# Four edits to the linear-attention stage of a hybrid decoder layer: the second pair's gate, the sum of x's two parts, the key transposes and the rule that hands out filler matmuls

## The chip, the cores and the metric

The kernel runs on one core of a Trainium2 chip. The metric is the device time of one execution in microseconds. Five engines work side by side, each in its own written order: TensorE (PE in the profile, with its weight loads as PEld), VectorE (DVE), ScalarE (ACT), GpSimd (POOL) and SyncE (SP), which issues nearly all DMAs.

## The reference

One decoder layer for 1024 prompt tokens and 64 sample tokens (8 sequences of 8), 1088 in all, in float32. Cut to what matters:

```python
xn   = rmsnorm(x, g_mix)
proj = xn @ w_in                      # qg kg vg r lr | qs ks vs
log_a = log_sigmoid(lr @ w_gup + b_g) / 16.0          # forget gate, 4 heads x 64 keys
S, o_g = gla_chunked(qg, kg, vg, log_a, s0, chunk)    # linear attention: S' = exp(b) S + k^T v
o_s  = dilated softmax attention of 8 heads (windows 128, 512, 2048)
o_g  = rmsnorm(o_g, g_gla) * silu(r)
h    = x + concat(o_g, o_s) @ w_out
y    = h + (silu(hn @ w_fg) * (hn @ w_fu)) @ w_fd      # hn = rmsnorm(h, g_ffn), width 2816
return rmsnorm(y, g_final), states, keys and values to keep
```

The gate's running sum `b = cumsum(log_a)` enters every product of queries and keys inside a chunk as `exp(b_t - b_s)`; the kernel cuts these products into levels, so that no exponent becomes large.

## The kernel before, in words

All products of float32 matrices are made of three matmuls on parts: a matrix is split into a high part `hi` (rounded by a copy) and a low part `lo` (the rest), and `mm3` (L201 to L203) adds hi·hi, hi·lo and lo·hi. `xhi` and `xlo` hold the transposed x in this way, 128 partitions by 8 blocks by 1088 tokens.

The program has these stages, with their times in the profiled execution: up to 60 us x is loaded, transposed and multiplied with the first two blocks of weights (queries and keys of the first pair of linear-attention heads); from 60 to about 310 us linear attention runs over two pairs of heads (`gla_heads`, g = 0 and 1); from about 310 to 675 us the softmax attention runs over four pairs (`attn_pair`, each about 88 us); then the output projection's second half and the norm, to about 780 us; then the feed-forward part to the end.

`gla_heads` walks three parts of the tokens: parts 0 and 1 are 512 prompt tokens each, part 2 the 64 sample tokens. In each part the levels h = 64, 32, 16, 8, 4, 2, 1 are gone through. A level takes two differences of `bT` on POOL (L618, L619), an exponent on ACT (L620), two products on DVE (tiles `Z`, L621, L622), and small matmuls on PE (L630 for the levels 64 and 32, L604 for the narrow ones, called bands). Then the state is brought forward: `kd` (POOL L647, ACT L649, DVE L650) is transposed on PE (L654), copied by ACT to `ktok` (L655), and multiplied with the values (L678). At the end of part 1 the outputs are scaled on DVE (L557) and transposed back (L692); part 2 has products of its own (L711, L713).

The gate (L366 to L381) is computed for both pairs ahead of `gla_heads(0)`: a matmul of `lrT` with `wg` (L371), then on DVE, ACT and again DVE to a scan (L380). Its tiles `z` and `mn` share two buffers (tag `qk`) with the queries and keys of the second pair, which a filler job writes later (L238).

Between these small matmuls PE is fed from a generator, `stream()`: 22 projection jobs of 12 steps of 6 matmuls each, then 32 steps of the output projection's first half. One step is called a yield here, and its matmuls filler. `tick` is called behind each level's, band's, state's and output's matmuls; it adds a weight from `GLA_W` and lets the generator run to a yield between `GLA_FROM[g]` and `GLA_TO[g]`, in proportion to the weights so far. Each of these pieces of filler may be issued only after the matmul it was called from (`issue_after`). Within these rules a scheduler that keeps a time line of its own sets the order of every engine's instructions.

x's parts are added again on POOL (L388) and written to `x_dram` by SP (L389), in pieces of 512, 512 and 64 tokens for each of 8 blocks, with two buffers, ahead of linear attention in the program and at low priority. The output projection reads `x_dram` much later (`xa`, from about 560 us on).

In the softmax attention SP's queue holds, for each pair, loads of a cache of keys (`in_cache_swa_k`), of values (`in_cache_swa_v`, in four tiles t = 0 to 3 with a small one per sequence), biases, and weights (`wraw`, L179) for the filler.

Of the kernel before, what the change touches and what calls it, by code (L numbers as in the profile page):

```python
# [2 lines left out]

# [1 line left out]

# [6 lines left out]
F32 = mybir.dt.float32  # L12
# [4 lines left out]
ALU = mybir.AluOpType  # L17
PSUM = bass.MemoryType.PSUM

P = 128  # L20
D = 1024
KT = D // P
# [3 lines left out]
TS = NB * NQ  # L26
TT = T + TS
# [10 lines left out]
NH = TT // 4  # L38
# [4 lines left out]
GLA_W = (1.0, 1.75, 0.75, 1.0)  # L43
# [60 lines left out]
def hymba_layer(  # L104
# [7 lines left out]
    nc = tc.nc  # L112
# [3 lines left out]
    pool = nc.gpsimd  # L116
    dma = nc.sync.dma_start
# [12 lines left out]
    x_dram = dram.tile([P, KT, TT], F32, name="x_dram")  # L130
# [9 lines left out]
    ident = const.tile([P, P], F32, name="ident")  # L140
# [65 lines left out]
    xhi = xpool.tile([P, KT, TT], F32R, name="xhi")  # L206
    xlo = xpool.tile([P, KT, TT], F32R, name="xlo")
# [142 lines left out]
    gla = open_pool("gla", side="left")  # L350
# [13 lines left out]
    pool.memset(reset[:, :T].rearrange("p (c t) -> p c t", t=P)[:, :, 0:1], 0.0)  # L364
    pool.memset(reset[:, T:].rearrange("p (c t) -> p c t", t=NQ)[:, :, 0:1], 0.0)
    bT = []  # L366
    for g in range(2):
        z = gla.tile([P, TT], F32, tag="qk", name="z", bufs=2)
        for c0, n in CHUNKS:
            ps = bank("S")  # L370
            mm(out=ps[:, :n], lhsT=wg[:, g * P : g * P + P], rhs=lrT[0:32, c0 : c0 + n], start=True, stop=True)  # L371
            vec.tensor_scalar(out=z[:, c0 : c0 + n], in0=ps[:, :n], scalar1=bg[:, g : g + 1], scalar2=None, op0=ALU.add)
        mn = gla.tile([P, TT], F32, tag="qk", name="mn", bufs=2)
        vec.tensor_scalar(out=mn, in0=z, scalar1=0.0, scalar2=None, op0=ALU.min)
        vec.scalar_tensor_tensor(out=z, in0=mn, scalar=2.0, in1=z, op0=ALU.mult, op1=ALU.subtract)
        act(out=z, in_=z, func=AF.Exp)
        act(out=z, in_=z, func=AF.Ln, bias=1.0)
        vec.tensor_tensor(out=mn, in0=mn, in1=z, op=ALU.subtract)
        b = gla.tile([P, TT], F32, tag="bT", name="bT", bufs=2)
        vec.tensor_tensor_scan(out=b, data0=reset, data1=mn, initial=0.0, op0=ALU.mult, op1=ALU.add)  # L380
        bT.append(b)  # L381


    with tc.high_priority(offset=-LOW):
        for k in range(KT):
            for lo, n in ((0, 512), (512, 512), (1024, TS)):
                xt = gla.tile([P, 512], F32, tag="xt", name="xt", bufs=2)[:, :n]
                pool.tensor_tensor(out=xt, in0=xhi[:, k, lo : lo + n].bitcast(F32), in1=xlo[:, k, lo : lo + n].bitcast(F32), op=ALU.add)  # L388
                dma(out=x_dram[:, k, lo : lo + n], in_=xt)  # L389

    ggh = gla.tile([P, 4], F32, name="ggh")
    vec.tensor_scalar(out=ggh, in0=gg, scalar1=0.5, scalar2=None, op0=ALU.mult)
# [144 lines left out]
    def gla_heads(g, q, k, V, Vs):  # L537
        ticks = [0]

        def tick(ins, kind):  # L540
            ticks[0] += GLA_W[kind]
            all_ = 20 * GLA_W[0] + 8 * GLA_W[1] + 2 * GLA_W[2] + 2 * GLA_W[3]
            fill_behind(ins, GLA_FROM[g] + (GLA_TO[g] - GLA_FROM[g]) * min(1, ticks[0] / all_))

        b = bT[g]
# [25 lines left out]
        for part in range(3):  # L571
            lo = part * W
            n = W if part < 2 else TS
            step = P if part < 2 else NQ
            ncmb = 4 if part < 2 else 1
            qp, kp, bp = q[:, lo : lo + n], k[:, lo : lo + n], b[:, lo : lo + n]
            levels = ((64, 32) if part < 2 else ()) + (LEVELS if part < 2 else LEVELS[2:])
            npart = P if part < 2 else TS
# [19 lines left out]
            def banded(ZL, ZR, mi):  # L598
                for i in range(2):
                    ps = columns(i, ncmb * 32)  # L600
                    for c in range(ncmb):
                        for j in range(nj):
                            sl = slice(c * P + 32 * j, c * P + 32 * j + 32)
                            ins = mm(out=ps[32 * j : 32 * j + 32, c * 32 : c * 32 + 32],  # L604
                               lhsT=ZL[64 * i : 64 * i + 64, sl], rhs=ZR[64 * i : 64 * i + 64, sl],
                               start=True, stop=True)
                    m = masks[:npart, mi, :].unsqueeze(1).broadcast_to([npart, ncmb, 32])
                    vec.copy_predicated(
                        out=comp[:, i * ncmb : (i + 1) * ncmb, :], mask=m.bitcast(U32),
                        data=ps[:npart].rearrange("p (x t) -> p x t", t=32),  # L610
                    )
                tick(ins, 0)

            for h in levels:
                Z = tmp("Z", 3)[:, :n]
                bv, zv = view(bp, h), view(Z, h)
                ref = bv[:, :, 0, h - 1 : h].broadcast_to([P, n // (2 * h), h])
                pool.tensor_tensor(out=zv[:, :, 0, :], in0=ref, in1=bv[:, :, 0, :], op=ALU.subtract)  # L618
                pool.tensor_tensor(out=zv[:, :, 1, :], in0=bv[:, :, 1, :], in1=ref, op=ALU.subtract)  # L619
                act(out=Z, in_=Z, func=AF.Exp, scale=1.0 / 16.0)  # L620
                vec.tensor_tensor(out=zv[:, :, 0, :], in0=view(kp, h)[:, :, 0, :], in1=zv[:, :, 0, :], op=ALU.mult)  # L621
                vec.tensor_tensor(out=zv[:, :, 1, :], in0=view(qp, h)[:, :, 1, :], in1=zv[:, :, 1, :], op=ALU.mult)  # L622
                if h <= 16:
                    banded(Z, Z, LEVELS.index(h))
                else:
                    for i in range(2):
                        pv = columns(i, ncmb * h).rearrange("p (x t) -> p x t", t=h)
                        for c in range(ncmb):
                            for a in range(0, P, 2 * h):
                                ins = mm(out=pv[a : a + h, c, :],  # L630
                                   lhsT=Z[64 * i : 64 * i + 64, c * P + a : c * P + a + h],
                                   rhs=Z[64 * i : 64 * i + 64, c * P + a + h : c * P + a + 2 * h],
                                   start=True, stop=True)
                        for a in range(0, P, 2 * h):
                            vec.tensor_copy(out=AT[a : a + h, i * ncmb : (i + 1) * ncmb, a + h : a + 2 * h], in_=pv[a : a + h])
                    tick(ins, 0)
            banded(kp, qp, len(LEVELS))
            for j in range(nj):
                act(out=AT[32 * j : 32 * j + 32, :, 32 * j : 32 * j + 32], in_=comp[32 * j : 32 * j + 32], func=AF.Copy)
# [5 lines left out]
            kd = tmp("kd")[:, :n]  # L645
            last = bp.rearrange("p (c t) -> p c t", t=step)[:, :, step - 1 : step].broadcast_to([P, n // step, step])
            pool.tensor_tensor(out=kd.rearrange("p (c t) -> p c t", t=step), in0=last,  # L647
                               in1=bp.rearrange("p (c t) -> p c t", t=step), op=ALU.subtract)
            act(out=kd, in_=kd, func=AF.Exp, scale=1.0 / 16.0)  # L649
            vec.tensor_tensor(out=kd, in0=kp, in1=kd, op=ALU.mult)  # L650
            kps = bank("T")
            ktok = tmp("ktok")
            for c in range(ncmb):
                nc.tensor.transpose(out=kps[:npart, c * P : c * P + P], in_=kd[:, c * P : c * P + npart], identity=ident)  # L654
            act(out=ktok[:npart, : ncmb * P], in_=kps[:npart, : ncmb * P], func=AF.Copy)  # L655

            ssg = gla.tile([P, 8], F32, tag="ssg", name="ssg", bufs=2)
# [106 lines left out]
    PF = {m: [att.tile([P, 2, P], F32, name=f"PF{i}{m}") for i in range(2)] for m in (P, 64)}  # L764
    for a in (Vf[0][64:, 1], Vf[1][64:, 1], PF[64][0][64:], PF[64][1][64:]):
        pool.memset(a, 0.0)

    def attn_pair(p):
        fs = slice(p * P, (p + 1) * P)
# [49 lines left out]
        ticks = [0]  # L819
# [85 lines left out]
        for gq in range(NTT // 2):  # L905
            Ps = [scores(2 * gq), scores(2 * gq + 1)]
            outputs(gq, Ps)
            for _ in range(4):
                next(sample, None)
        for _ in sample:  # L910
# [545 lines left out]
```

## Time and profile before

| what | value |
|---|---|
| three runs | 1564.93, 1574.18, 1579.67 us (median 1574.18) |
| the profiled execution | 1570.21 us |
| its span, and TensorE's mean granted clock | 1568.4 us, 0.973 |
| PE busy | 1476.7 us (94%), 13459 matmuls |
| DVE busy | 989.7 us (63%) |
| ACT busy | 593.1 us (38%) |
| POOL busy | 587.3 us (37%) |

The profiled execution lies 1.8 us above its span and 4 us below the median of the three runs. Busy shares are means over stages that differ: PE is close to full in the feed-forward part and has most of its gaps in linear attention, between 90 and 125 us and around 145 and 246 us, and near 680 us. The granted clock stands in the profile's window view as a share of 2.4 GHz; 0.50 is 1.2 GHz.

### The profile page before, as it was taken

The page shows a single profiled execution, that of the slowest core. Times are in us where ns is not written, and L with a number is a line of the kernel's source. Part 1 is how long each engine was busy: PE and PEld are TensorE (multiplying, and loading weights), DVE is VectorE, ACT ScalarE, POOL GpSimd, SP SyncE. Part 2 cuts the span into 40 slices and gives each one's busy share as a digit, 9 for nine tenths or more (in the row PEclk, how much of TensorE's full clock was granted, in tenths as well). Part 3 has the DMA queues.
Part 4 walks back from the last instruction along what each step waited for, and adds up shares of the span by engine and source line. Part 5 has one row for each costly group of instructions (what it writes and reads, how often), then busy time and mean ns, then how long its engine had stood idle before and what let it go on. Part 6 is the DMA issues. An engine that isn't in the chain of part 4 may idle for free. (4 is left out here: it accounts for less than half of the span.)

```text
span 1568.4 us, 32306 instructions
## 1 busy us (share of the span) xinstructions
PE 1476.7 (94%) x13459; PEld 1328.9 (85%) x13459; DVE 989.7 (63%) x1669; ACT 593.1 (38%) x1006; POOL 587.3 (37%) x413
## 2 busy tenths in 40 slices
PE   6979999999999999969889999999988999999996
PEld 6867877886777766569889999999988999999996
DVE  5486586543233324246577777777788887767766
ACT  4143233245242526323443333333335433333432
POOL 1494342041212010024475543345543455444521
PEclk9988999999999999989999999999999999999998
DMA  5321121164443527575543332232332633323211
GB/s 156 90 81 31 30 70 43 43 189 117 125 116 110 156 89 228 151 230 165 174 132 95 108 94 81 82 108 83 108 110 91 185 95 108 94 81 100 90 41 58
DMA packets 242211, 170.23 MB, mean 109 GB/s; under 512 B 17648, under 2 KB 228496, under 8 KB 242064
## 3 DMA queue, kind: packets, MB, share of 16 engines
q1 hardware_dynamic: 237856, 167.95, 36.0%
q8 instruction: 106, 1.74, 0.5%
q10 hardware_dynamic: 4208, 0.21, 0.2%
q14 instruction: 41, 0.34, 0.1%
HBM read 144.66 MB, written 23.46 MB: 107 GB/s over the span
## 5 line engine op out<-in xcount | busy, mean ns | idle before, releaser
L1113 POOL TENSOR_TENSOR raw<-raw 128x1024 f32<-128x1024 f32 x88 | 260.6, 2969 | 366.2 <-DVE wlo L173 242.2
L172 ACT ACTIVATE whi<-raw 128x1024 fp32r<-128x1024 f32 x154 | 162.7, 1058 | 236.6 <-PE ps_a L1225 84.1
L173 DVE TENSOR_TENSOR wlo<-raw,whi 128x1024 fp32r<-128x1024 f32 x154 | 242.3, 1574 | 4.7 <-ACT whi L172 4.7
L201 PE MATMUL ps_d<-ghi,wdhi 128*128 128x272 f32 (+2 forms) x704 | 203.0, 290 | 6.2 <-DVE B L1190 4.3
L202 PE MATMUL ps_d<-glo,wdhi 128*128 128x272 f32 (+2 forms) x704 | 203.4, 290 | 1.1 <-DVE glo L173 1.1
L201 PE MATMUL ps_mm<-xhi,whi 128*128 128x384 f32 (+1 forms) x576 | 198.9, 346 | 2.0 <-ACT whi L172 1.6
L203 PE MATMUL ps_d<-ghi,wdlo 128*128 128x272 f32 (+2 forms) x704 | 200.2, 289 | 0.0
L203 PE MATMUL ps_mm<-xhi,wlo 128*128 128x384 f32 (+1 forms) x576 | 196.0, 341 | 1.4 <-DVE wlo L173 1.4
L202 PE MATMUL ps_mm<-xlo,whi 128*128 128x384 f32 (+1 forms) x576 | 194.3, 338 | 0.2 <-DVE xlo L278 0.2
L1225 PE MATMUL ps_b<-xhi,wlo 128*128 128x272 f32 x528 | 156.9, 297 | 3.9 <-DVE wlo L173 3.6
L1225 PE MATMUL ps_b<-xhi,whi 128*128 128x272 f32 x528 | 155.2, 294 | 2.4 <-ACT whi L172 1.0
L1225 PE MATMUL ps_b<-xlo,whi 128*128 128x272 f32 x528 | 154.4, 292 | 0.8 <-DVE xlo L173 0.8
L201 PEld LDWEIGHTS ps_d<-ghi,wdhi 128*128 128x128 f32 x704 | 133.1, 189 | 7.2 <-DVE B L1190 4.7
L202 PEld LDWEIGHTS ps_d<-glo,wdhi 128*128 128x128 f32 x704 | 133.5, 190 | 1.5 <-DVE glo L173 1.5
L203 PEld LDWEIGHTS ps_d<-ghi,wdlo 128*128 128x128 f32 x704 | 131.8, 189 | 0.0
L201 PEld LDWEIGHTS ps_mm<-xhi,whi 128*128 128x128 f32 x576 | 110.1, 191 | 12.9 <-issue 8.2
L203 PEld LDWEIGHTS ps_mm<-xhi,wlo 128*128 128x128 f32 x576 | 110.3, 192 | 9.3 <-issue 6.6
L1277 DVE TENSOR_TENSOR h<-h,ps_d 128x544 f32<-128x544 f32 x168 | 113.5, 711 | 3.0 <-PE ps_d L203 3.0
L202 PEld LDWEIGHTS ps_mm<-xlo,whi 128*128 128x128 f32 x576 | 110.5, 192 | 5.5 <-issue 4.7
L1225 PE MATMUL ps_a<-xhi,whi 128*128 128x272 f32 x352 | 102.3, 291 | 7.2 <-DVE h L1277 3.8
L1225 PEld LDWEIGHTS ps_b<-xhi,wlo 128*128 128x128 f32 x528 | 101.9, 193 | 6.2 <-DVE wlo L173 4.5
L1225 PEld LDWEIGHTS ps_b<-xhi,whi 128*128 128x128 f32 x528 | 101.9, 193 | 3.6 <-ACT whi L172 1.2
(363 smaller groups left out, 3490.0 us busy)
## 6 DMA issues: line engine op xcount, KB each, us to landing
raw<-in_w_ffn_gate_dram SPq DMA_DIRECT2D x88, 256.0 KB, 3.1
raw<-in_w_ffn_up_dram SPq DMA_DIRECT2D x88, 256.0 KB, 3.5
wd_raw<-in_w_ffn_down_dram SPq DMA_DIRECT2D x44, 512.0 KB, 3.7
wraw<-in_w_in_dram SPq DMA_DIRECT2D x22, 512.0 KB, 4.2
raw<-in_cache_swa_k_dram SPq DMA_DIRECT2D x32, 256.0 KB, 4.7
raw<-in_cache_swa_v_dram SPq DMA_DIRECT2D x32, 256.0 KB, 3.9
wraw<-in_w_out_dram SPq DMA_DIRECT2D x16, 512.0 KB, 4.7
xa<-x_dram SPq DMA_DIRECT2D x48, 136.0 KB, 3.3
```

Of the source, the lines that this page charges most:

```text
L172: a = by.tensor_copy(out=hi, in_=raw) if by else act(out=hi, in_=raw, func=AF.Copy)
L173: return a, vec.tensor_tensor(out=lo, in0=raw, in1=hi.bitcast(F32), op=ALU.subtract)
L201: mm(out=ps, lhsT=whi[k], rhs=xhi[k], start=first and k == 0, stop=False)
L202: mm(out=ps, lhsT=whi[k], rhs=xlo[k], start=False, stop=False)
L203: mm(out=ps, lhsT=wlo[k], rhs=xhi[k], start=False, stop=last and k == n - 1)
L1113: add = lambda out, a, b, op: pool.tensor_tensor(out=out, in0=raw[a], in1=raw[b], op=op)
L1225: mm(out=banks[bk][:, s], lhsT=l[:, k, s], rhs=r, start=first and k == 0 and a == 0, stop=k == n - 1 and a == 2, skip_group_check=not first)
L1277: ins = vec.tensor_tensor(out=hk, in0=hk, in1=ps, op=ALU.add)
```

## The change

Four edits, all in or around linear attention:

1. The gate becomes a function `forget_gate(g)`; the first pair's is called as before, the second's with low priority, so that its instructions may be placed later.
2. x's parts are added in the first two pairs of the softmax attention instead of ahead of linear attention: `x_rows(k)` is called after each step `gq` of pairs 0 and 1 and adds four pieces of 272 tokens, 32 in all, with a single buffer, each followed by its store.
3. The key transposes may be issued only after the last matmul of level 32 (`early`).
4. In `tick`, the sample part's levels and bands count twice, and the sum of all weights is 24 level weights in place of 20 (41.5 in place of 37.5).

```diff
+    def forget_gate(g):
         z = gla.tile([P, TT], F32, tag="qk", name="z", bufs=2)
...
+    forget_gate(0)
     with tc.high_priority(offset=-LOW):
-        for k in range(KT):
-            for lo, n in ((0, 512), (512, 512), (1024, TS)):
-                xt = gla.tile([P, 512], F32, tag="xt", name="xt", bufs=2)[:, :n]
-                pool.tensor_tensor(out=xt, in0=xhi[:, k, lo : lo + n].bitcast(F32), in1=xlo[:, k, lo : lo + n].bitcast(F32), op=ALU.add)
-                dma(out=x_dram[:, k, lo : lo + n], in_=xt)
+        forget_gate(1)
...
-            ticks[0] += GLA_W[kind]
-            all_ = 20 * GLA_W[0] + 8 * GLA_W[1] + 2 * GLA_W[2] + 2 * GLA_W[3]
+            ticks[0] += GLA_W[kind] * (2 if part == 2 and kind == 0 else 1)
+            all_ = 24 * GLA_W[0] + 8 * GLA_W[1] + 2 * GLA_W[2] + 2 * GLA_W[3]
             fill_behind(ins, GLA_FROM[g] + (GLA_TO[g] - GLA_FROM[g]) * min(1, ticks[0] / all_))
...
+            early = None
             for h in levels:
...
                     tick(ins, 0)
+                    early = ins
...
-            for c in range(ncmb):
-                nc.tensor.transpose(out=kps[:npart, c * P : c * P + P], in_=kd[:, c * P : c * P + npart], identity=ident)
+            with tc.issue_after(early.ins) if early else nullcontext():
+                for c in range(ncmb):
+                    nc.tensor.transpose(out=kps[:npart, c * P : c * P + P], in_=kd[:, c * P : c * P + npart], identity=ident)
...
+    def x_rows(k):
+
+        for lo in range(0, TT, NH):
+            xt = att.tile([P, NH], F32, tag="xt", name="xt", bufs=1)
+            pool.tensor_tensor(out=xt, in0=xhi[:, k, lo : lo + NH].bitcast(F32), in1=xlo[:, k, lo : lo + NH].bitcast(F32), op=ALU.add)
+            dma(out=x_dram[:, k, lo : lo + NH], in_=xt)
...
             outputs(gq, Ps)
+            if p < 2:
+                x_rows(4 * p + gq)
```

On PE, in part 0 of the first pair, before: the key transposes stand ahead of the matmuls of level 32 (32x32 here).

```order
L630 MATMUL ps_S<-Z 64x64 x8
L201 MATMUL ps_mm<-xhi,whi 128x384
L202 MATMUL ps_mm<-xlo,whi 128x384
L203 MATMUL ps_mm<-xhi,wlo 128x384
L201 MATMUL ps_mm<-xhi,whi 128x384
L202 MATMUL ps_mm<-xlo,whi 128x384
L203 MATMUL ps_mm<-xhi,wlo 128x384
L654 MATMUL ps_T<-ident,kd 128x128 x4
L630 MATMUL ps_S<-Z 32x32 x16
```

And in the changed kernel, where L630 is L629 and L654 is L655:

```order
L629 MATMUL ps_S<-Z 64x64 x8
L201 MATMUL ps_mm<-xhi,whi 128x384
L202 MATMUL ps_mm<-xlo,whi 128x384
L203 MATMUL ps_mm<-xhi,wlo 128x384
L201 MATMUL ps_mm<-xhi,whi 128x384
L202 MATMUL ps_mm<-xlo,whi 128x384
L203 MATMUL ps_mm<-xhi,wlo 128x384
L629 MATMUL ps_S<-Z 32x32 x16
L655 MATMUL ps_T<-ident,kd 128x128 x4
```

The two rows have changed places; the filler between is the same.

On PE at the border from the first pair to the second (the last groups of part 1's outputs, then the sample part's L712 and L714, then the transposes of the scaled outputs, L693), in the changed kernel:

```order
L668 MATMUL ps_A<-V,AT 64x128 x2
L672 MATMUL ps_A<-S,qE 64x128 x2
L629 MATMUL ps_S<-Z 64x64 x8
L668 MATMUL ps_X<-V,AT 64x128 x2
L672 MATMUL ps_X<-S,qE 64x128 x2
L712 MATMUL ps_A<-Vs,AT 64x128
L714 MATMUL ps_A<-S_863,qm 64x128 x4
L712 MATMUL ps_A<-Vs,AT 64x128
L714 MATMUL ps_A<-S_863,qm 64x128 x4
L629 MATMUL ps_S<-Z 32x32 x16
L693 MATMUL ps_T<-ident,otok 128x128 x8
L201 MATMUL ps_mm<-xhi,whi 128x384
```

Before, 72 filler matmuls stood between the last transposes of values (L420, three rows further up) and the transposes of the scaled outputs (L692): 28 among the last groups of L667 and L671, 14 ahead of the first L711 and 30 behind the last L713. Now none stands there, and the filler starts again behind L693.

On SP in the first pair of the softmax attention, in the changed kernel, where L774 is the new store, L936 and L940 the cache loads, L928 the sample bias, L179 weights for the filler and L909 a store of outputs:

```order
L936 DMA raw<-in_cache_swa_v_dram 128x4x128 x2
L774 DMA x_dram<-xt 128x272 x3
L936 DMA raw<-in_cache_swa_v_dram 128x4x128
L909 DMA o_dram<-sum 128x256
L936 DMA raw<-in_cache_swa_v_dram 128x4x128
L774 DMA x_dram<-xt 128x272
L936 DMA raw<-in_cache_swa_v_dram 128x4x128 x2
L774 DMA x_dram<-xt 128x272 x3
L928 DMA sb<-in_bias_s_dram 128x832
L936 DMA raw<-in_cache_swa_v_dram 128x4x128 x2
L179 DMA wraw<-in_w_in_dram 128x8x128
```

The new stores stand between the loads; each waits for its add on POOL, and the next add waits for the buffer, which is free when the store has landed.

## Rows read from the trace of the kernel before

**Rows 1.** Windows: length, busy us (instructions) of PE, PEld, DVE, ACT, POOL; clock; DMA.

```profile
60.00:100.00 40.00, 37.54 (x219) 32.64 (x217) 24.69 (x31) 12.92 (x18) 33.57 (x29) 1.00 0.39 121
100.00:124.00 24.00, 16.91 (x409) 13.92 (x409) 22.84 (x36) 9.26 (x12) 23.95 (x23) 0.72 0.16 59
...
140.00:152.00 12.00, 9.35 (x200) 7.30 (x197) 9.60 (x31) 3.73 (x12) 3.85 (x6) 0.72 0.01 3
...
244.00:252.00 8.00, 5.14 (x106) 4.58 (x107) 7.52 (x23) 1.00 (x3) 4.69 (x6) 0.57 0.08 30
...
sum 240.00, PE 222.37 PEld 188.21 DVE 162.88 ACT 79.69 POOL 111.03; mean PE 27.80 PEld 23.53 DVE 20.36 ACT 9.96 POOL 13.88
```

**Rows 2.** Waits of PE, 60 to 310 us: total, times, longest.

```profile
PE ps_T L654 <- DVE kd L650: 6.3, 1, 6.3
PE ps_S L630 <- DVE AT L635: 4.5, 2, 3.1
PE ps_S L604 <- DVE comp L608: 2.2, 2, 1.9
...
PE ps_T L720 <- DVE osm L557: 1.0, 1, 1.0
```

**Rows 3.** DVE's groups, 88.05 to 104.58 us: busy and mean ns, idle before.

```profile
L622 DVE TENSOR_TENSOR Z<-qT,Z 128x256 f32<-128x256 f32 x3 | 4.2, 1401 | 0.0
L621 DVE TENSOR_TENSOR Z<-kT,Z 128x256 f32<-128x256 f32 x3 | 3.1, 1032 | 1.2 <-ACT Z L620 1.2
...
L650 DVE TENSOR_TENSOR kd<-kT,kd 128x512 f32<-128x512 f32 x1 | 1.7, 1747 | 0.0
...
L375 DVE SCALAR_TENSOR_TENSOR z<-mn,z 128x1088 f32<-128x1088 f32 x1 | 1.4, 1409 | 0.0
L374 DVE TENSOR_SCALAR mn<-z 128x1088 f32<-128x1088 f32 x1 | 1.1, 1133 | 0.0
```

**Rows 4.** Time line of DVE: start, duration, instruction, idle before.

```profile
107.67 2.87 DVE L380 TENSOR_TENSOR_SCAN bT<-reset,mn 128x1088 f32<-128x1088 f32 x1
110.55 0.56 DVE L238 SCALAR_TENSOR_TENSOR qk<-ps_mm,rstd_bc 128x384 f32<-128x384 f32 x1
...
171.97 0.42 DVE L622 TENSOR_TENSOR Z<-qk,Z 128x256 f32<-128x256 f32 x1
...
186.37 0.29 DVE L674 COPY otok<-ps_X 128x128 f32<-128x128 f32 x1 [0.96 <-PE ps_X L671]
...
194.51 1.23 DVE L557 TENSOR_TENSOR otok<-otok,rs 128x1024 f32<-128x1024 f32 x1
```

**Rows 5.** ACT's groups, 99 to 108 us.

```profile
L377 ACT ACT_TABLE_LOAD x1 | 1.3, 1283 | 0.0
L620 ACT ACT_TABLE_LOAD x1 | 1.3, 1283 | 0.0
L377 ACT ACTIVATE z<-z 128x1088 f32<-128x1088 f32 x1 | 1.1, 1111 | 0.0
```

**Rows 6.** PE at the pairs' border: time line, then a group of 186.3 to 196.5 us.

```profile
189.20 0.43 PE L711 MATMUL ps_A<-Vs,AT 128*64 128x128 f32 x2
...
190.13 1.09 PE L713 MATMUL ps_A<-S,qm 128*64 128x128 f32 x10
...
L630 PE MATMUL ps_S<-Z 64*64 64x64 f32 (+1 forms) x17 | 0.9, 211 | 0.0
```

**Rows 7.** The tile `xt`: durations of its adds, and its stores' landing.

```profile
L388 POOL TENSOR_TENSOR xt<-xhi,xlo x24: 315/1292/3757, 61.6 to 123.9; 128x512 f32<-128x512 f32 x16, 128x64 f32<-128x64 f32 x8
...
DMA to landing us min/median/max: 1.4/2.0/3.4
```

**Rows 8.** SP's time line in the first attention pair.

```profile
350.75 0.54 SPq L179 DMA_DIRECT2D wraw<-in_w_in_dram  x1
...
386.62 0.37 SPq L926 DMA_DIRECT2D raw<-in_cache_swa_v_dram  x1
```

**Rows 9.** Waits of PE, 310 to 860 us.

```profile
PE ps_mm L201 <- ACT ohi L172: 10.0, 1, 10.0
```

## What the change was predicted to do

> **What bounds the kernel now.** I read the shares first: TensorE is busy for 94% of the span, so an edit can win only where PE stands still or runs at its lower clock. I then cut the stretch that the edits touch into windows [rows 1]. From 60 to 300 us PE is busy 222.37 of 240 us, so 17.6 us are idle. The granted clock is below 1.00 in three of these windows, each time behind a gap: 16.91 us of work at a mean of 0.72, 9.35 at 0.72 and 5.14 at 0.57, that is 2.4 GHz for part and 1.2 GHz for part of each. Work at full clock would have taken 16.91 × 0.72 and so on, so the clock costs 4.7 + 2.6 + 2.2 = 9.5 us. Idle time and clock together are **27 us, the most that linear attention can give back**. The waits of PE [rows 2] then say what ended the gaps: 6.3 us once for `kd` ahead of the key transposes, 4.5 us in two waits for `AT` copies, 2.2 us for `comp`, 1.0 us for `osm`.
>
> Why was `kd` late? It is written on DVE, and DVE's groups from the first gate's scan to `kd` [rows 3] show the reader two things: the second gate's L374 and L375 stand in the middle (1.1 and 1.4 us), and the six products `Z` take 7.3 us, 1.0 to 1.4 us each, where the same product takes 0.42 us at 171.97 [rows 4]. In that stretch POOL was busy without a pause (23.95 of 24 us from 100 to 124 us [rows 1]), with x's sums among its work [rows 7].
>
> **The change part by part.**
>
> *Gate late, sums gone, transposes behind level 32 (60 to 128 us).* In the profile `kd` comes 16.5 us after the scan. Off go L374 and L375 (2.5), one of the gate's evacuations (0.5), the slowness of six products (7.3 − 6 × 0.42 = 4.8), about 1 us of `kd` itself and DVE's wait of 1.2 [rows 3]: some 8 to 10 us, so `kd` is there near 96 us instead of 104.6. The 16 matmuls of level 32 now stand ahead of the transposes, so the 6.3 us wait goes. With it go the wait for `comp` (2.2) and the clock loss behind both (4.7): 13.2 us. What is late next? The second gate now runs in the midst of the narrow bands. On ACT its table load, its logarithm and the table load back (1.3 + 1.1 + 1.3 = 3.7 us [rows 5]) stand ahead of the copy of `ktok` and the next exponents; before, they fell into PE's wait. About 0.8 of it is covered by the band's matmuls, 2.9 is not. And the scan of the second gate still frees the buffer for the second pair's queries (at 110.55 the evacuation L238 follows the end of the scan at once [rows 4]); I put that scan's end near 108 (`kd` at 96, then 2.5 us of L374 and L375, 3.5 on ACT, and some 5.5 for L378, two bands' copies and products, and the scan). That is under three us earlier than 110.5, while PE arrives some eight earlier, so a filler chunk waits some 2 us (two chunks of that job stand ahead and use up the rest). 13.2 − 4.9 gives **−8 us**; the bounds are −14 (all idle and clock loss of the two first windows, 2.5 + 7.1 + 4.7) and −3 (only half of the key wait, with the rest moved).
>
> The GPSIMD Engine Reference of the Trainium skill ("8. Key points") says that GpSimd shares its SBUF interfaces with VectorE and contends with instructions that have two SBUF inputs. The trace agrees, with 1.4 us in place of 0.42. By that rule the levels' own subtractions on POOL would go on slowing the products, and this term would be −6.
>
> *The same stage, part 1 (140 to 152 us).* The two products and copies ahead of its first wait are the same, and no more filler stands there: 0.
>
> *The border of the pairs.* Here the new weights take filler away. With 41.5 in place of 37.5 the yields come later, and those that used to fall under part 1's outputs now hang on a matmul behind the border: by the order, none of 72 filler matmuls is left there. What PE then has to wait for is DVE's chain from the last copy of outputs at 186.37 to the end of L557 at 195.74 [rows 4], 9.4 us. Of PE's own work 2.0 us (189.20 to 191.22) and 0.9 us lie in it [rows 6], and one evacuation of 0.5 leaves DVE. So 6.0 us of idle, which the trace of before doesn't show because filler covered it. Behind a gap comes the lower clock: the two later windows lost 2.6 and 2.2 us for gaps of 2.7 and 2.9 us [rows 1]. **+8 us**, between +4 (waits that overlap the chain, no clock loss) and +13 (the whole chain, the clock, and two more waits among output groups).
>
> *Second pair (240 to 252 us).* Filler that was moved back now stands ahead of the wait for `AT` there, 27 matmuls by the order. At 0.17 us each (37.54 us for 219 matmuls, mostly filler, in the first window [rows 1]) that is 4.6 us, enough for the 3.1 us wait [rows 2]. Of 2.9 idle and 2.2 clock I take **−4** (0 to −5). The wait for `osm` (1.0) is covered as well: **−1**.
>
> *Tail of the attention.* The 10.0 us wait for `ohi` [rows 9] hangs on the last sample outputs, transposed by PE between filler. Of that filler now 43 matmuls precede the last transposes by the order (24 before), so those come later, and less is left to cover the wait: 19 × 0.12 us (272 columns, by 0.17 for 384) = **+2** (−1 to +4).
>
> *x's sums in the attention.* POOL has room (it is busy for 37% of the span). What counts is SP, whose stores stand between loads, with one buffer: add, issue, landing, then the next add. The add takes 1.29 × 272/512 = 0.7 us, the issue 0.3, the landing 2.0 [rows 7]: 3.0 us. Eleven stores stand from the filler's weights at 350.75 to the last value tile at 386.62 [rows 8], so 35.9 / 11 = 3.26 us are there for each. It just fits; I take **+1** (0 to +4).
>
> Edits with one answer: the feed-forward part keeps its order on all engines, 0; the adds' total on POOL is the same, and POOL bounds nothing there, 0.
>
> Sum: −8 + 8 − 4 − 1 + 2 + 1 = **−2 us**. Against the profiled execution's 1570.2 that is 1568.2. The median of the runs is 4 us higher, and by it 1572. I say **1570**.
>
> **The rivals.**
>
> *Stores hold up the attention (slower).* With one buffer, a landing of 3.4 us, the longest seen [rows 7], makes the cycle 4.4 us. Eleven stores then take 48 us where 36 are there, and the value tile behind them comes 12 us late, in each of two pairs; PE's sample products stand in written order and wait. That is +24 less the +1 in the sum: about 1592. It decides from a landing of 2.3 us on (cycle above 3.26). For it: the attention moves far more data than linear attention. Against it: the median landing of 2.0 leaves room, and filler may precede the waiting products. Chance 0.13.
>
> *The border costs little (faster).* If the chain at the border runs faster without filler's evacuations, and POOL free of sums lets the first stretch recover all, the terms are −14, +2, −5, −1, 0 and 0: −18, so 1553. For it: POOL and DVE are both full in the worst stretch. Against it: L557 follows on its chain, whose instructions don't depend on filler. Chance 0.2.
>
> *The first stretch hardly gains.* The gate is late, but the wait goes over to the second pair's queries, a filler chunk that PE must run in order: −3 instead of −8, and the border at +12. Sum +7, 1577 to 1580. This is also the case in which double weights do not put filler behind the samples of the first pair. Chance 0.17. The remaining 0.5 are my forecast, 1562 to 1577.
>
> **How the numbers follow.** What a measurement of this kernel can tell from no change is about 1%, 16 us. Faster by more than that is below 1558: most of the second rival (0.14) and a few hundredths of the forecast, 0.18. Slower is above 1590: most of the first rival and a little of the third, 0.14. Same: 0.68. The range takes the forecast, the third rival, and the near parts of the other two: 1554 to 1588.
>
> **What would show it.** Right: the wait for `kd` is gone from PE's list; products `Z` near 0.5 us between 94 and 103 us; a new idle stretch of 5 to 8 us ahead of the transposes of the scaled outputs, ended by L557, with a clock of about 0.5 behind it; the wait of 3.1 us near 246 gone. Wrong: waits for the value cache above 2 us in pairs 0 and 1, a gap near 110 us ended by L238, or a full PE at the border.

## The result, and the profile after

The changed kernel takes 1584.72 us (median of 9 runs, 1580.86 to 1588.45) where the one before takes 1574.18. The ratio is **1.0085, 95% interval 1.0070 to 1.0101**: slower by 13 us by the ratio (the two medians lie 10.5 us apart), within the 1% that the prediction called "same", inside its range, but on the other side of no change than its −2 us. The profiled execution took 1588.23 us with a span of 1586.4, 18.0 above the one before; so the two profiles lie further apart than the medians.

The windows of the changed kernel, to be read against [rows 1] (length, then busy time of PE, PEld, DVE, ACT, POOL, granted clock, DMA share, GB/s). The last row is the whole of linear attention:

```profile
60.00:100.00 40.00, 38.77 (x257) 34.55 (x256) 26.26 (x39) 13.34 (x18) 12.29 (x14) 1.00 0.19 51
100.00:124.00 24.00, 18.88 (x406) 16.39 (x405) 15.74 (x34) 8.99 (x12) 12.11 (x15) 0.93 0.01 2
124.00:152.00 28.00, 25.35 (x511) 19.95 (x510) 19.43 (x58) 11.84 (x33) 11.03 (x16) 0.94 0.13 36
170.00:184.00 14.00, 8.05 (x101) 6.27 (x102) 12.16 (x40) 4.07 (x16) 6.04 (x9) 0.74 0.14 39
184.00:200.00 16.00, 16.00 (x204) 12.34 (x206) 11.04 (x32) 4.11 (x9) 4.47 (x6) 0.91 0.15 35
240.00:250.00 10.00, 3.23 (x224) 2.66 (x224) 9.81 (x23) 2.60 (x4) 6.59 (x7) 0.75 0.34 111
250.00:260.00 10.00, 9.70 (x237) 8.02 (x237) 5.02 (x20) 3.95 (x10) 2.29 (x8) 0.74 0.01 3
...
60.00:310.00 250.00, 227.99 (x3064) 192.86 (x3063) 153.75 (x404) 79.61 (x189) 76.03 (x98) 0.95 0.14 38
```

The first stretch got better: 100 to 124 us has 5.1 us of idle instead of 7.1 and a clock of 0.93 instead of 0.72. In exchange there are two stretches with holes: 170 to 184 us, full before (6.0 idle, clock 0.74, and still 0.91 behind), and 240 to 250 (6.8 idle, 0.75), where one wait of 3.1 us stood before. In all, linear attention now leaves 22.0 us idle, 17.6 before. The border before:

```profile
170.00:184.00 14.00, 14.00 (x132) 10.44 (x133) 8.30 (x27) 6.75 (x22) 5.11 (x7) 1.00 0.15 43
184.00:200.00 16.00, 16.00 (x162) 14.33 (x160) 13.47 (x49) 4.17 (x12) 4.76 (x8) 1.00 0.01 2
```

The waits of PE from 60 to 310 us (total, times, longest), against [rows 2]:

```profile
PE ps_S L629 <- DVE AT L634: 5.0, 3, 2.9
PE ps_S L602 <- DVE comp L606: 3.4, 2, 2.0
PE ps_T L679 <- ACT ktok L656: 3.1, 1, 3.1
PE ps_T L693 <- DVE otok L555: 2.5, 1, 2.5
PE ps_A L712 <- ACT AT L639: 2.5, 1, 2.5
PE ps_S L602 <- DVE sp L157: 1.6, 1, 1.6
```

The 6.3 us for `kd` are gone. New are `ktok` (3.1), `AT` at the border (2.5 of ACT's L639, and 2.9 of the 5.0 in the first row), and in the second pair `comp` (2.0), `sp`, a value of the norm (1.6), and the outputs' scaling (`otok`, L555, was L557; 2.5).

From 310 to 860 us, against [rows 9]:

```profile
PE ps_mm L201 <- ACT ohi L172: 10.0, 1, 10.0
PE ps_X L991 <- DMA raw<-in_cache_swa_v_dram: 9.9, 2, 5.3
```

The value cache makes PE wait 9.9 us in two waits, 5.3 us in pair 0 and 4.5 us in pair 1. Before, the same line was:

```profile
PE ps_X L981 <- DMA raw<-in_cache_swa_v_dram: 2.0, 3, 0.9
```

The windows of the first two attention pairs (their ends moved with the pairs), in the changed kernel and then before:

```profile
330.00:426.00 96.00, 90.32 (x917) 67.38 (x916) 31.17 (x95) 37.28 (x88) 37.17 (x46) 0.96 0.54 156
426.00:519.00 93.00, 88.09 (x880) 64.16 (x879) 27.98 (x87) 35.39 (x80) 25.38 (x29) 0.98 0.48 139
```

```profile
330.00:418.00 88.00, 86.76 (x895) 63.63 (x894) 29.80 (x92) 36.03 (x86) 21.28 (x25) 1.00 0.51 141
418.00:505.00 87.00, 86.18 (x878) 62.79 (x877) 27.79 (x87) 35.59 (x80) 15.30 (x16) 1.00 0.45 126
```

So 5.7 and 4.9 us are idle, and the clock is below 1.00 behind each wait. Before, both pairs had the clock at 1.00 and 1.2 and 0.8 us idle.

Time lost to idle and clock, added up in windows of about 4 us (20 in the feed-forward part) between the same places of the two programs, shows where the 18.0 us of the profiles are (idle + loss by clock):

| stretch, to its end before / after | before | after | difference |
|---|---|---|---|
| start, 60 us | 13.0 + 1.4 | 12.3 + 0.0 | −2.1 |
| first stretch, 124 | 9.6 + 4.9 | 6.3 + 1.4 | −6.8 |
| part 1 of the first pair, 152 | 2.6 + 2.6 | 2.6 + 1.5 | −1.1 |
| border, 200 | 0.0 + 0.0 | 5.9 + 3.5 | +9.4 |
| to 240 | 1.8 + 0.0 | 0.0 + 0.0 | −1.8 |
| second pair, 262 | 3.1 + 2.3 | 7.1 + 3.2 | +4.9 |
| to 310 | 0.5 + 0.0 | 0.0 + 0.0 | −0.5 |
| attention pairs 0 and 1, 505 / 519 | 2.0 + 0.0 | 10.6 + 3.5 | +12.1 |
| pair 2, 590 / 604 | 1.2 + 0.0 | 1.3 + 0.0 | +0.1 |
| to the feed-forward part, 775 / 790 | 22.5 + 7.5 | 22.5 + 10.3 | +2.8 |
| feed-forward part | 35.3 + 10.4 | 36.0 + 12.0 | +2.3 |

The rest, −1.3, is work at full clock and rounding. The feed-forward part has the same order in both kernels, so its row and the first say how far single profiles differ by themselves.

### The profile page after: what moved, and what is told of

Same layout as the page of the kernel before. It is cut to its first block, busy times and chain, and to the rows that moved or that the text cites. A ratio compares the mean times of both kernels' runs of the same rounds, so it can differ in the third digit from the quotient of the medians.

```text
span 1586.4 us, 32354 instructions
## 1 busy us (share of the span) xinstructions
PE 1481.8 (93%) x13459; PEld 1334.0 (84%) x13459; DVE 972.7 (61%) x1669; ACT 591.9 (37%) x1006; POOL 574.2 (36%) x421
## 4 chain that ended last, share of the span: by engine, by line
PE 71%; DVE 11%; DMA 10%; ACT 3%; issue 2%; POOL 1%; SPq 1%; DVEq 0%; ACTq 0%; POOLq 0%
PE ps_b L1235 11%; PE ps_a L1235 7%; PE ps_c L1235 6%; PE ps_mm L201 6%; PE ps_mm L203 6%; PE ps_mm L202 6%; PE ps_d L203 5%; PE ps_d L202 5%; PE ps_d L201 5%; DVE wlo L173 3%; DMA x_dram<-xt 2%; DMA wraw<-in_w_out_dram 2%; PE ps_S L847 2%; PE ps_X L991 1%; PE ps_A L896 1%
```

## The experiments

Ratios are to the kernel before, run on the same chip in the same session; its median in the three sessions was 1571.4 to 1572.0 us, so a ratio of 1.0085 is 1585 there. 0.1% is 1.6 us. The change itself was run in the session of the result only, so a difference between its ratio and another's goes by way of the kernel before; each of the two has an interval of about ±0.15 to 0.2%.

**The fourth edit undone, the others kept.**

```diff
-            ticks[0] += GLA_W[kind] * (2 if part == 2 and kind == 0 else 1)
-            all_ = 24 * GLA_W[0] + ...
+            ticks[0] += GLA_W[kind]
+            all_ = 20 * GLA_W[0] + ...
```

> The change with its fourth edit undone (weights and their sum as before; gate late, sums in the attention and transposes behind level 32 stay). By the order, all 72 filler matmuls are back at the border of the pairs, and 18 among the second pair's bands. Theory A (the change lost time at two places: about 13 us in the attention pairs 0 and 1, where SP's stores hold up the value loads, and about 10 + 4 us in the two holes that the weights leave, less some 7 won in the first stretch): the two holes go, the attention's loss stays, so 1574 to 1579 us on the scale on which the change takes 1585 and the one before 1574; PE waits of about 10 us for the value cache stay. Theory B (the attention lost nothing of its own, it only took over filler that the holes had left undone): near 1567, and the waits for the value cache shrink to about 2 us.

1577.11 us, ratio 1.0047 (1.0029 to 1.0066). Theory B, near 1567, falls. Theory A allowed 6 to 11 us under the change and 0 to 5 above the kernel before; it is 6 under (0.38%) and 7 above, so what theory A expected in the trace is there, and the gain is at the low end of it or under. The two holes are gone from the trace. Here are the border and the second pair:

```profile
170.00:200.00 30.00, 28.97 (x310) 23.92 (x309) 22.55 (x75) 10.34 (x33) 9.92 (x14) 1.00 0.08 21
240.00:252.00 12.00, 8.90 (x194) 7.33 (x197) 10.80 (x29) 2.86 (x8) 5.73 (x6) 0.86 0.18 65
```

The border has 1.0 us idle at full clock, and 240 to 252 us has the 3.1 us that it had before. The attention keeps its waits for the value cache (10.2 us in three).

**The second edit undone, the others kept** (x's sums ahead of linear attention again).

```diff
+        for k in range(KT):
+            for lo, n in ((0, 512), (512, 512), (1024, TS)):
+                xt = gla.tile([P, 512], F32, tag="xt", name="xt", bufs=2)[:, :n]
...
-            if p < 2:
-                x_rows(4 * p + gq)
```

> The change with its second edit undone (x's sums ahead of linear attention again, two buffers; the rest of the change stays). Theory A: the waits for the value cache fall from 9.9 to about 2 us and the attention's 13 us go; the sums slow the first stretch by 0 to 6 us; 1572 to 1578 us. Theory B: the attention stays as long as in the change, the first stretch gets slower: 1585 to 1590.

1579.82 us, ratio 1.0051 (1.0032 to 1.0071): above the expected upper end of 1578, but 5 us under the change. Pairs 0 and 1 have 1.5 us of idle again and the clock at 1.00. What went wrong with the estimate is the first stretch: 6.6 idle and 10.1 by the clock, 16.7 in place of the change's 7.7.

**The whole change, x's stores on POOL's queue.**

```diff
-            dma(out=x_dram[:, k, lo : lo + NH], in_=xt)
+            pool.dma_start(out=x_dram[:, k, lo : lo + NH], in_=xt)
```

> The whole change, but x's stores in the attention are issued by POOL's own queue instead of SP's. The single buffer stays, so sum and store still follow each other, but no load stands behind them. Theory A (SP's in-order queue is what hurts): waits for the value cache about 2 us, 1570 to 1575 us. Rival (the bytes of the stores themselves, 4.5 MB among the loads, delay the value tiles): the waits stay near 10 us and the time near 1585.

1575.95 us, ratio 1.0029 (1.0014 to 1.0044): 0.56% under the change, one microsecond above theory A's range and nine under the rival's 1585. PE's waits for the value cache are as short as before:

```profile
PE ps_X L991 <- DMA raw<-in_cache_swa_v_dram: 2.3, 3, 1.0
```

The bytes, the single buffer and the number of stores are the same; only the queue differs. What SP waits for from 345 to 400 us, first in this kernel, then in the changed one from 350 to 400 us:

```profile
SPq L936 <- PE ps_T L947: 16.0, 6, 9.4
SPq L928 <- PE ps_T L980: 7.3, 1, 7.3
```

```profile
SPq L774 <- POOL xt L773: 17.2, 9, 4.7
SPq L774 <- POOL qbd L791: 2.5, 1, 2.5
```

On POOL's queue the stores hold nobody up, and SP again waits for room alone, as it did before (15.0 and 7.3 us): it is ahead of what PE needs. In the change it waits for sums at its stores, and every load behind them comes as much later. The stores even land later from POOL's queue, at a median of 3.0 us against 1.9; it doesn't matter there.

**The fourth edit alone.**

> The kernel before with the fourth edit alone (weights). By the order it has the two holes of the change. Theory A: about 10 us of idle and low clock at 170 to 200 us and 4 more at 240 to 250, little given back elsewhere: 1582 to 1588 us. Rival (filler that is put off fills other gaps and comes back): 1574 to 1577.

1577.42 us, ratio 1.0040 (1.0025 to 1.0056): less than theory A, just above its rival. The holes are there in full (9.7 us at the border, 9.2 in the second pair, 40.0 in linear attention as a whole against 27.5). Taking the edit away from the change won 0.38%, and from the stores on POOL's queue (above) to the next experiment it is 0.42%: some 6 us, in three comparisons. In the last two the traces agree with the time: the holes hold 13.9 and 11.8 us more with the fourth edit, but the rest of linear attention loses less (the first stretch alone 3.2 and 2.5 us), so that linear attention as a whole loses 7.4 and 6.4 us more. Here, with the fourth edit alone, it loses 12.5 us more, and half of it doesn't show in the time. The stretch from pair 3 to the feed-forward part has 2.2 us less of idle and clock loss, which is part of it; for the rest the trace names no place, and single profiles differ by as much.

**Edits 1 to 3 with POOL's stores** (weights as before).

> Edits 1 to 3 (gate late, sums in the attention, transposes behind level 32), weights as before, and x's stores on POOL's own queue. If the losses are the two holes of the weights and SP's queue, and nothing else, both are away and the gain of the first stretch is left: linear attention at 24 us of idle and clock loss (27.5 before), the attention's first two pairs at 2 us, so 3 to 6 us under the kernel before, 1565 to 1568 where that takes 1571. If the stores cost the attention something that SP's queue does not explain, it is 1571 to 1577.

1568.27 us, ratio 0.9987 (0.9972 to 1.0001). With both places mended the loss is gone; a gain of 2 us is not clear of noise, and less than expected.

**The second edit alone, stores on SP.**

> The kernel before with the second edit alone (x's sums and stores in the attention, on SP, one buffer). If SP's queue is the cause, the waits for the value cache stand at about 10 us and pairs 0 and 1 lose some 12 us, less what linear attention wins without the sums on POOL (0 to 7 us): 1576 to 1584 where the kernel before takes 1571. If the loss needs the other edits (filler that comes late), it is 1566 to 1573.

1579.35 us, ratio 1.0055 (1.0035 to 1.0075). The attention's loss doesn't need the other edits: 8.8 us of waits for the value cache, 14.4 us of idle and clock loss in pairs 0 and 1. And in the first stretch this edit alone brings 14.5 down to 7.9 us, with the wait for `kd` gone.

**Weights doubled, their sum as before** (on the kernel before).

```diff
-            ticks[0] += GLA_W[kind]
+            ticks[0] += GLA_W[kind] * (2 if part == 2 and kind == 0 else 1)
             all_ = 20 * GLA_W[0] + 8 * GLA_W[1] + 2 * GLA_W[2] + 2 * GLA_W[3]
```

> The kernel before with the sample part's weights doubled, but the sum of weights as before (20 level weights in place of 24). By the order the filler of parts 0 and 1 stands as before, with 57 matmuls instead of 44 around the sample part's products at the border, and none is taken away from it. If edit 4's loss comes from the larger sum, which thins out the filler of parts 0 and 1, this is within 3 us of the kernel before, 1568 to 1574. If the double weights themselves cost the time, it is as slow as edit 4 alone, near 1577.

1570.18 us, ratio 0.9985 (0.9970 to 1.0001). It is the larger sum that costs, not the double weight: against the fourth edit alone, which differs in the sum only, this is 0.55% faster. 24 in place of 20 spreads the same filler over more ticks, and parts 0 and 1 of each pair get less.

**Edits 1 and 3 alone.**

> Edits 1 and 3 alone (gate late, transposes behind level 32; sums ahead of linear attention, weights as before). If the first stretch gains because POOL's sums are gone, it keeps waits of 4 us and more there and takes 1569 to 1575. If the late gate and the place of the transposes are what counts, idle and clock loss from 60 to 124 us fall from 14.5 to about 8 and the time is 1564 to 1568.

1571.13 us, ratio 0.9998 (0.9986 to 1.0010), the time of the first case, though no single wait there is above 2.5 us. In its profile the idle time of the first stretch falls to 6.4 us, but the clock takes 10.4 (the profiled execution took 1578.98 us, the longest of its 13 runs): by themselves the late gate and the later transposes win nothing.

**The second edit alone, POOL's stores.**

> The kernel before with the second edit alone, its stores on POOL's own queue. Theory C (of the four edits only the move of the sums wins something, 6 to 7 us of idle and clock loss in the first stretch, and SP's queue took it away): linear attention at about 24 us of loss, attention pairs 0 and 1 at about 2, and 1563 to 1567 where the kernel before takes 1571 to 1572. If the late gate and the later transposes are needed for a gain, it is 1569 to 1573.

1574.95 us, ratio 1.0020 (1.0006 to 1.0034): theory C falls, and the time lies above the other case too. Linear attention loses 24.1 us (27.5 before) and pairs 0 and 1 lose 2.2, as expected, but this kernel isn't faster. From pair 3 to the feed-forward part 31.4 us are lost against 30.0, with a wait of 12.5 us for `ohi` (10.0 before).

**The same with weights doubled, sum as before.**

> As the run above, with the sample part's weights doubled and the sum of weights as before. The doubled weights alone moved the time by less than 3 us, so 1562 to 1567 by theory C; 1568 and more if the order of filler at the border costs what the sums win.

1573.18 us, ratio 1.0009 (0.9996 to 1.0023): the second case by its time, but not for the reason given there, as PE has no idle time at the border (152 to 200 us) in this trace.

**All four edits with both places mended.**

> All four edits with the two places mended: stores on POOL's queue, weights doubled for the samples with the sum of weights as before. If the two mended places are the whole loss, 1565 to 1569 where the kernel before takes 1571 to 1572, as with the first three edits and POOL's stores. If edits 1 and 3 cost something of their own, it lies 2 us or more above the run above.

1566.01 us (1561.12 to 1570.38), ratio **0.9959 (0.9943 to 0.9975)**: faster than the kernel before and the fastest of all. Its linear attention leaves 15.1 us idle:

```profile
60.00:310.00 250.00, 234.87 (x3118) 198.28 (x3117) 162.37 (x411) 82.12 (x192) 81.23 (x101) 0.97 0.15 40
```

Pairs 0 and 1 have 1.0 and 1.4 us idle at full clock, and the wait for `ohi` is 8.6 us. So edits 1 and 3 do win something beside the other two: without them it was 1.0009. With the weights as before they make 0.9987 of 1.0020 on POOL's queue, but on SP's only 1.0047 of 1.0055, which isn't clear of noise, and by themselves they win nothing.

**The second edit alone, stores on SP in half pieces.**

```diff
-        for lo in range(0, TT, NH):
-            xt = att.tile([P, NH], F32, tag="xt", name="xt", bufs=1)
+        for lo in range(0, TT, NH // 2):
+            xt = att.tile([P, NH // 2], F32, tag="xt", name="xt", bufs=2)
```

> The second edit alone, stores on SP, in pieces of 136 tokens with two buffers of half the size (the same room, twice as many stores; sum and store of two pieces overlap). If the time that SP stands at a store is the chain through one buffer (sum, issue, landing), the waits for the value cache fall from about 9 us to under 4 and the time to 1568 to 1575. If the number of stores among the loads or their bytes count, the waits stay near 9 us or grow, and the time is 1578 or more.

1578.83 us, ratio 1.0046 (1.0028 to 1.0065); waits for the value cache 11.8 us. The second case, but it doesn't clear the chain: from 350 to 400 us SP still waited 14.7 us for sums in 12 waits. Two stores land nearly together, then both buffers are filled again, so the sum and the landing overlap little. A second buffer of full size was not tried, so it stays open whether the stores could stay on SP with their sums made earlier.

## Why the prediction was wrong

Its sum was −2; the profiles say +18, the ratio +13. Two of its terms failed, a third came only in part, and a fourth agrees by luck.

**"It just fits; I take +1."** This is the step that failed most. The term measures +12 in the profiles, which alone turns the sum of −2 to +9, and, by the stores moved to POOL's queue, 0.56% or 9 us in time (0.60% beside the other weights, 0.35% with the second edit alone). With this place alone mended the change is still slower than the kernel before (1.0029), and with the weights alone put back it is too (1.0047); with both, nothing is lost (0.9987). The cycle was right as long as nothing disturbs it, and wrong where it counts. POOL's sums in the changed kernel (start, duration, idle before):

```profile
379.00 0.77 POOL L773 TENSOR_TENSOR xt<-xhi,xlo 128x272 f32<-128x272 f32 x1 [1.89 <-DMA x_dram<-xt]
381.70 0.76 POOL L773 TENSOR_TENSOR xt<-xhi,xlo 128x272 f32<-128x272 f32 x1 [1.94 <-DMA x_dram<-xt]
387.44 0.76 POOL L773 TENSOR_TENSOR xt<-xhi,xlo 128x272 f32<-128x272 f32 x1 [4.97 <-DMA x_dram<-xt]
390.10 0.76 POOL L773 TENSOR_TENSOR xt<-xhi,xlo 128x272 f32<-128x272 f32 x1 [1.90 <-DMA x_dram<-xt]
```

And SP beside it:

```profile
382.49 0.32 SPq L774 DMA_DIRECT2D x_dram<-xt  x1
382.90 1.05 SPq L936 DMA_DIRECT2D raw<-in_cache_swa_v_dram  x2
388.23 5.63 SPq L774 DMA_DIRECT2D x_dram<-xt  x3
393.96 0.37 SPq L928 DMA_DIRECT2D sb<-in_bias_s_dram  x1
394.42 0.96 SPq L936 DMA_DIRECT2D raw<-in_cache_swa_v_dram  x2
```

The cycle is 2.7 us (predicted 3.0) from 379.00 to 381.70, and 5.7 behind it, where two value tiles of 256 KB each are issued beside the store: that store, issued at 382.49, has landed when the next sum starts at 387.44, 4.9 us later. The same stands at two other stores with two value tiles beside them, issued at 371.91 and 475.54: the next sum waits until 4.4 and 4.0 us after the issue. Then three stores stand in a row, and the seventh of the eight value tiles, issued at 386.62 before [rows 8] (the prediction took it for the last; the eighth was issued at 387.64), goes out at 394.42. PE, in order, stands still:

```profile
398.47 0.66 PE L991 MATMUL ps_X<-raw,pT 128*32 128x128 f32 x8 [5.32 <-DMA raw<-in_cache_swa_v_dram]
```

The landing's median is 1.9 us, as taken from [rows 7], but its longest is 5.0, and with a single buffer the loads behind the store paid for the longest. The first rival had this mechanism, place and direction, at a chance of 0.13. Its own test, a landing from 2.3 us on, fails by the median of 1.9 and holds at the stores that count (4.0 to 4.9); its price of 24 us took a long landing for every store and is twice what came. Also wrong was the argument that the budget of 3.26 us is there for each store: a mean over 36 us says nothing of the last three, which follow each other right ahead of the load that PE needs (388.23 to 393.86 in pair 0, and 480.35 to 485.94 in pair 1). That large loads slow the stores' landing is what fits these rows; it wasn't varied by itself. The Trainium skill, "DMA: Bandwidth & Descriptors", "Latency and other measured facts", gives HBM's latency as 0.2 us on average and 2 us at high load. The trace agrees in direction, 1.9 against 4.9 us to landing.

**"Filler ... now stands ahead of the wait for `AT` there" (−4).** The 27 matmuls did cover that wait. But they were the filler that had stood among the next bands: by the order, 18 matmuls lay between the level-32 matmuls and the outputs' transposes before, and none does now. PE waits there for `comp`, `sp` and `otok` instead (2.0 + 1.6 + 2.5 us), and the term is +4.9. The step looked at the first wait and not at what came behind it. The fourth edit's four terms (+8, −4, −1, +2) together make +5, near the 6 us that it costs in time; that is luck, as the −4 is wrong by 9 us.

The other terms:

| term | predicted | in the profiles | what shows it |
|---|---|---|---|
| first stretch | −8 | −6.8 | mechanism as predicted: `kd` ready at 95.7 us (96 predicted); the wait for `ktok` 3.1 us (2.9); the second gate's scan ends at 110.0 (108), and no filler chunk of the second pair's queries makes PE wait over 0.5 us |
| part 1 of the first pair | 0 | −1.1 | clock |
| border | +8 | +9.4 | no filler there; outputs' last copy at 173.45 to the end of L555 at 183.47, 10.0 us (9.4); the idle time is three waits beside this chain, two for `AT` (2.5 and 2.9) and 0.6 at the transposes, not one ahead of them |
| wait for `osm` | −1 | −1.8 | the wait is gone, with it 0.7 us for `AT` in the same stretch (200 to 240 us) |
| tail | +2 | +2.8 | luck: the wait for `ohi`, which was to grow, is 10.0 us in both, and idle time is 22.5 in both; the difference is the clock's |

The first stretch in the change shows the reader a cure that worked. DVE's groups ahead of `kd`, against [rows 3]:

```profile
L621 DVE TENSOR_TENSOR Z<-qT,Z 128x256 f32<-128x256 f32 x3 | 1.7, 550 | 0.0
L620 DVE TENSOR_TENSOR Z<-kT,Z 128x256 f32<-128x256 f32 x3 | 1.6, 521 | 1.2 <-ACT Z L619 1.2
...
L650 DVE TENSOR_TENSOR kd<-kT,kd 128x512 f32<-128x512 f32 x1 | 0.7, 677 | 0.0
```

The products take 0.52 to 0.55 us instead of 1.0 to 1.4 on average, with POOL busy 12.29 of 40 us instead of 33.57. One by one they show it too: 0.74 and 0.83 us at 89.09 and 89.76, while POOL does the levels' subtractions, 0.41 each from 93.10 to 94.63, with POOL idle, and 0.84 and 1.25 at 101.85 and 102.61, beside POOL again. The rule of the Trainium skill's GPSIMD Engine Reference ("8. Key points") that the prediction weighed is borne out by this. By it the term was −6, as near to −6.8 as the −8.

But the prediction put the gain down to three edits at once. Alone, the sums' move brings the first stretch from 14.5 to 7.9 us, while with the late gate and the later transposes alone it is 16.8 in the profile. And −6.8 is the most that any kernel with edits 1 to 3 shows: with POOL's stores, other weights or both (four kernels) the first stretch loses 8.9 to 11.5 us, 3.0 to 5.6 less than before, the clock making most of the difference. In time, edits 1 to 3 with POOL's stores are only 2 us faster (0.9987, not clear of noise), so the −8 came in part.

The border term, +9.4 in the profile, is not what the time shows: the fourth edit, with both of its holes, costs 6 us in three comparisons. In two of them the rest of linear attention gives 5 to 7 us back by the traces; in the third, the edit alone, what gives the rest back isn't settled. The runs also part the edit in two. The larger sum costs more than the edit, 0.55% (fourth edit alone against the doubled weights with the old sum) and 0.70% (POOL's stores, 1.0029 against 0.9959); the double weight with the old sum wins 0.11 to 0.28% in three pairs of runs (1 to 0.9985, 1.0020 to 1.0009, 0.9987 to 0.9959), of which only the last is clear of noise by itself.

By the runs the change is made up of 0.38 to 0.42% for the fourth edit, 0.56 to 0.60% for SP's queue, and −0.13% for all the rest. That these add up to the 0.85% measured follows from how they are taken; what the runs show is that the first two cost the same in either order. Open is why the sums' move on POOL's queue alone is no faster (1.0020), though its linear attention lost 3.4 us less, and is faster together with edits 1 and 3 (0.9987 and 0.9959). The wait for `ohi` goes along with it (12.5 us alone, 8.1 and 8.6 together), but nothing was tried there.

## What to carry to other kernels

A store whose data comes late is badly placed on the in-order queue that brings the next stage's loads: one wait there delays all of them (here 9 us in time for 32 stores). Its price is read from the longest landing with the loads in flight, at the last few stores ahead of the load that is needed, and not from a median and a mean budget. Filler has a fixed amount: before booking a gain where more of it stands, look where it was taken from, up to the next place where every engine waits for one chain; and doubling a weight in one place must leave the sum that the others are divided by alone, or it thins them out (here 0.55 to 0.70%).

## What the runs showed that was not expected

A store of 136 KB issued from POOL's queue lands after 3.0 us (median; 2.0 to 5.6), from SP's after 1.9 (1.7 to 5.0), and occupies the issuing engine for 0.56 us instead of 0.33; the kernel with POOL's was the faster one all the same.

The same first stretch with the same sort of idle time lost very different amounts to the clock from one kernel to the next: 1.4 us with 6.3 idle in the change, 10.1 with 6.6 when the sums were put back, 10.4 with 6.4 in edits 1 and 3 alone. It isn't only the scatter of single profiles: the two kernels with the late gate and x's sums ahead agree with each other (10.1 and 10.4), and the three with the second edit alone and the weights as before lose 4.3 us each. Kernels with edits 1 to 3 lose 1.4 to 5.9. So a term for the clock can't be carried over from the profile of another kernel, even with the same idle time; why the losses differ so much was not looked into.
